# Regrouping the matmul order of a 32-expert block by tile width: one block of full-width work per expert, the sums of a pair as one block, 32-column work ahead of 64-column work in the down projection

## The chip, the cores and the metric

The kernel runs on one core of one Trainium2 chip. The metric is the device time of one execution in microseconds (us). A core has a matmul engine (TensorE, PE in the profile; its weight loads are listed as PEld), three engines for vectors and scalars (VectorE or DVE, ScalarE or ACT, GpSimd or POOL), and SyncE (SP), whose queue issues nearly all loads here. Each engine works through its own queue in order; between engines there are semaphores. The PE writes only to PSUM, eight banks of 512 float32 per partition, and the DVE or the ACT takes the results out.

## The reference, cut to what matters

The program is one layer of a hybrid encoder for 512 tokens of width 1024. A pooling mixer and a differential attention, then a cross-attention, then a mixture of 32 experts (each token goes to four) are added to `x`; a last RMSNorm follows. The change touches only the experts:

```
logits = xt @ w_router + b_router
top_val, top_idx = lax.top_k(logits, 4);  gates = softmax(top_val)
for each expert e, for the tokens that chose it:
    gate, up = split(xb @ w_gu[e] + b_gu[e])
    hb = (min(up, 7) clipped at -7, + 1) * min(gate, 7) * sigmoid(1.702 * gate)
    y[token] += (hb @ w_down[e] + b_down[e]) * gate_weight
```

## The kernel before

**What one expert is.** The kernel gives each expert 96 places (`CAP`); experts with more tokens are finished by a loop at the end (`overflow`), which does nothing in this run. The first 64 places are worked on in matmuls with 64 stationary columns, two of which stand side by side in the array (one fills PSUM partitions 0 to 63, the other 64 to 127). The last 32 places are worked on in matmuls with 32 stationary columns, four side by side. Experts with at most 64 tokens skip most of the 32-column work: the PE branches on a flag (`when`, line 102; `cond()` in the code). All else uses the full 128 columns: gathering a token list (`slots`), turning activations (`xgT`, `actT`), adding biases, and the sums into `x` (`comb`).

**What an iteration of `experts` does.** In iteration `e` of the loop the PE works on gate and up of expert `e` and on the down projection of expert `e - 1`:

- `load_gate_up(e + 1)` and `load_down(e)` put twelve loads of 1 MB on the SP queue, into a pool of 17 buffers.
- `biases` starts the accumulators with the biases: `gu1` (64 places, tile `pa`, a *pair* of two banks) and `gu2` (32 places, tile `pc`, one bank). Both are printed as `gu`.
- `gate_up1(j)`, for `j` from 0 to 7, adds one eighth of the contraction to `gu1` with four 64-column matmuls. Each is recorded as two instructions in the profile, so `x8` there is one `j`.
- `gate_up2(k)` does the same for the 32 places. It stands after `j = 3` (for `k` 0 to 3) and after `j = 7` (for `k` 4 to 7).
- Amid the `j` steps stand, at full width: after `j = 2` `dispatch(e + 2)` (`slots`), after `j = 6` `turn_act` of expert `e - 1` (`actT`), and in odd iterations after each of `j` = 3, 4, 5, 6 one `combine`, which multiplies the weighted results of a *pair* of experts with one-hot matrices for 128 tokens at a time (six matmuls into `comb`) and has the DVE add the sum into `x` (`add_sums`, line 1171 before). There are four such sums for each pair, one for each 128 tokens.
- `swiglu` (lines 1059 to 1065) turns `gu1` and `gu2` into activations on DVE and ACT.
- `to_features` of expert `e + 1` (`xgT`, then two DVE multiplications into `xT`) stands at the end of the gate and up part.
- `down` of expert `e - 1` runs half of its 64-column matmuls (`first(0)`), then its 32-column ones (`second`), then the other half (`first(1)`). ACT and DVE split each result into a high and a low part (lines 120 and 121).

**What sets the order.** On the PE the order is that of the Python code (`queued`, `in_order`): each matmul is issued after the one before it in the program. The other engines' orders are the framework's, which follows readiness.

**PSUM.** Pool `ps1` has four single banks, for `slots`, `actT` (two of them), `gu2`, and the down projection's `down1` and `down2`. Pool `ps2` has two pairs of banks, for `gu1`, `xgT` and `comb`. From the biases to `swiglu`, `gu1` holds one of the two pairs.

Of the kernel before, what the change touches and what calls it, by code (L numbers as in the profile page):

```python
# [23 lines left out]
NT = S // P  # L24
KT = D // P
MEM = 256
NE = 32
# [33 lines left out]
class Block:  # L61
# [1054 lines left out]
    def down(self, aT, aT2, dn, gat, tok, cond, a, c, last=False):  # L1116


        (ya, oha), (yb, ohc) = a, c
        nc, mw = self.nc, self.mw  # L1120
        pd = [self.bank("down1") for _ in range(2)] if last else [self.bank("down1")] * 2
        pe = self.bank("down2", (P, 256))

        def first(h):
            for c in range(4):
                w = dn[2 * h + c // 2]
                for o in range(2):
                    k = D * (c % 2) + 512 * o
                    self.mm(pd[o][64 * o:64 * o + 64], aT[:, c, 64 * h:64 * h + 64], w[:, k:k + 512],
                            start=h == 0 and c == 0, stop=h == 1 and c == 3, skip_group_check=True)  # L1130

        def second(q, b):
            for o in range(4):
                k = D * b + 256 * o
                self.mm(pe[32 * o:32 * o + 32], aT2[:, b, 32 * q:32 * q + 32], dn[q][:, k:k + 256],
                        start=q + b == 0, stop=q == 3 and b == 1, skip_group_check=True)

        nc.vector.tensor_scalar(oha, self.iota_t, tok[:, 0:1], None, op0=OP.is_equal)
        nc.vector.tensor_scalar(ohc, self.iota_t[0:64], tok[0:64, 1:2], None, op0=OP.is_equal)
        if not last:  # L1140
            first(0)
        second(0, 0)
        with cond():
            for k in range(1, 8):
                second(k // 2, k % 2)
        for q in range(4):
            r, c = slice(32 * q, 32 * q + 32), slice(256 * (q % 2), 256 * (q % 2) + 256)
            self.split(yb[0:32, q // 2, c], yb[32:64, q // 2, c], pe[r], scale=gat[r, 1:2])
        if last:
            first(0)  # L1150
        first(1)
        for h in range(2):
            r = slice(64 * h, 64 * h + 64)
            self.split(ya[0:64, h], ya[64:P, h], pd[h][r], scale=gat[r, 0:1])
# [18 lines left out]
    def experts(self):  # L1173
# [7 lines left out]
            return [t[:, 0] for t in disp[e][1:]]  # L1181

        xTs[0] = self.first_features()
        acts, parts = {}, {}
        pick = self.pick.rearrange("p v h q e -> p (v h q) e")
        for e in range(NE + 1):

            if e < NE:
                gu = self.gu.pop(e)
                cond = lambda e=e: self.when(self.flag(e))  # L1190
                if e == 0:
                    biases = self.load_down_biases()
                if e + 1 < NE:
                    self.load_gate_up(e + 1)
                    if e:
# [4 lines left out]
                for j in range(KT):  # L1200
                    self.gate_up1(pa, xT, gu[j], j)
                    if e == 0 and j == 0:
                        self.count()
                    if e == 0 and j == 1:
                        disp[1] = self.dispatch(1, 1)
                        gather(1)
                    if j == 3 or e == 0 and j in (1, 5):
                        with cond():
                            for k in range(j - 1 if e == 0 else 0, j + 1):
                                self.gate_up2(pc, xT, gu[k], k)  # L1210
                    if j in (3, 4, 5, 6) and e % 2 and e > 2:
                        self.combine(j - 3, parts[e // 2 - 1])
                    if j == 2 and e + 2 < NE:
                        disp[e + 2] = self.dispatch(e + 2, 1)
                    if j == 5 and e == 0:
                        disp[0] = self.dispatch(0, 1)
                        biases = self.round_down_biases(biases)
                    if e == 1 and j == 2:
                        biases = self.down_biases(biases)
                    if e == 1 and 2 < j < 7:  # L1220
                        self.combine(j - 3, [biases])
                    if j == 6 and e >= 1:
                        aT = [self.turn_act(t, n) for t, n in zip(acts.pop(e - 1), (4, 2))]
                    if j == 6 and e + 1 < NE:
                        xg = self.normed(xgs.pop(e + 1))
                if e:
                    act = self.swiglu(pa[:, 0], pa[:, 1], 512)
                with cond():
                    for k in range(4 if e else 6, KT):
                        self.gate_up2(pc, xT, gu[k], k)  # L1230
                if e == 0:
                    xTs[1] = self.to_features(xg)
                    act = self.swiglu(pa[:, 0], pa[:, 1], 512)
                acts[e] = act, self.swiglu(pc[:, 0], pc[:, 1], 256)
                if 0 < e < NE - 1:
                    xTs[e + 1] = self.to_features(xg)
            else:
                aT = [self.turn_act(t, n) for t, n in zip(acts.pop(e - 1), (4, 2))]

            if e:  # L1240
                f = e - 1
# [159 lines left out]
```

## Time and profile before

| | |
|---|---|
| time, median of 3 runs | 1530.17 us (1529.25 to 1530.84) |
| time of the profiled execution | 1531.06 us |
| span of its instructions | 1529.3 us |
| granted TensorE clock, mean over the span | 0.989 |
| PE busy | 1482.5 us, 97% |
| DVE, ACT, POOL busy | 695.2, 385.1, 39.0 us |
| read from HBM | 449.45 MB, 297 GB/s over the span |

The expert loop takes the span from about 390 us (biases of expert 0) to about 1500 us. [...]

### The profile page before, as it was taken

Reading aid. Unit: us, or ns where it says so; the run is one execution under the profiler, and the core shown is the slowest. Engines: PE = TensorE matmul, PEld = TensorE weight load, DVE = VectorE, ACT = ScalarE, POOL = GpSimd, SP = SyncE. Lnnn points to the kernel's source line nnn. Section 1 sums busy time; section 2 is a strip of 40 time slices with the busy share of each in tenths; the row PEclk is TensorE's granted clock in tenths of the full one; section 3 lists DMA queues with packets and bytes.
Section 4 is the critical chain, followed back from the end, with each engine's and each line's share of the span. In section 5 each row is a group of like instructions: output and inputs, shape, how many; then the busy total and the mean of one; then the engine's idle time right before and its main releaser. Section 6 shows DMA issues by size and latency. Waiting matters only on the chain. (4 is left out here: it accounts for less than half of the span.)

```text
span 1529.3 us, 22025 instructions
## 1 busy us (share of the span) xinstructions
PE 1482.5 (97%) x8852; PEld 748.6 (49%) x8852; DVE 695.2 (45%) x1679; ACT 385.1 (25%) x691; POOL 39.0 (3%) x52
## 2 busy tenths in 40 slices
PE   8999999999999999999999999999999999999994
PEld 7878788888433333434333333333343433433332
DVE  6858865543353433335343334344343433444234
ACT  5346644441111111121211112121111112121113
POOL 0000000000000000000000000000000000000001
PEclk9999999999899999999999999999999999999997
DMA  6222225148778998989999998899989999999901
GB/s 221 90 86 88 106 63 175 80 196 318 273 304 341 387 398 318 369 356 373 396 405 408 407 381 344 343 400 367 395 342 386 387 393 370 364 396 387 416 25 57
DMA packets 84153, 455.38 MB, mean 298 GB/s; under 512 B 14169, under 2 KB 14690, under 8 KB 34882
## 3 DMA queue, kind: packets, MB, share of 16 engines
q1 hardware_dynamic: 79170, 438.90, 72.9%
q0 software_dynamic: 3472, 12.29, 2.5%
q10 hardware_dynamic: 1392, 2.51, 0.4%
q8 instruction: 87, 1.43, 0.4%
q14 instruction: 32, 0.26, 0.0%
HBM read 449.45 MB, written 4.21 MB: 297 GB/s over the span
## 5 line engine op out<-in xcount | busy, mean ns | idle before, releaser
L107 PE MATMUL gu<-gu,xT 128*64 128x512 f32 (+1 forms) x3200 | 602.7, 598 | 1.3 <-PEq L102 1.3
L107 PEld LDWEIGHTS gu<-gu,xT 128*64 128x64 f32 (+1 forms) x3200 | 167.7, 127 | 344.2 <-issue 337.3
L107 PE MATMUL down<-dnw,aT 128*32 128x256 f32 (+1 forms) x2288 | 305.3, 478 | 3.3 <-PEq L102 2.5
L107 PEld LDWEIGHTS down<-dnw,aT 128*32 128x32 f32 (+1 forms) x2288 | 109.1, 122 | 175.3 <-issue 149.6
L1105 ACT ACTIVATE aT<-actT 128x512 f32<-128x512 f32 x64 | 27.9, 487 | 542.2 <-PE actT L111 542.2
L1171 DVE TENSOR_TENSOR x<-comb,x 128x1024 f32<-128x1024 f32 x68 | 82.9, 1221 | 131.6 <-PE comb L107 131.6
L1059 DVE TENSOR_SCALAR g<-gu 128x256 f32<-128x256 f32 (+1 forms) x64 | 33.3, 554 | 229.1 <-PE gu L107 193.5
L121 DVE SCALAR_TENSOR_TENSOR yb<-down,gat,yb 32x256 fp32r<-32x256 f32 x128 | 61.6, 481 | 129.4 <-ACT yb L120 129.4
L120 ACT ACTIVATE yb<-down,gat 32x256 fp32r<-32x256 f32 x128 | 59.7, 466 | 224.3 <-PE down L107 118.2
L107 PE MATMUL comb<-ya,yb 128*128 128x512 f32 x256 | 97.0, 420 | 3.7 <-PEq L102 2.8
L107 PEld LDWEIGHTS comb<-ya,yb 128*128 128x128 f32 x256 | 47.9, 187 | 63.3 <-DVE x L1171 37.8
L118 DVE TENSOR_TENSOR w_lo<-w,w_hi 128x1024 fp32r<-128x1024 f32 x56 | 67.0, 1219 | 7.5 <-ACT w_hi L117 7.2
L121 DVE SCALAR_TENSOR_TENSOR ya<-down,gat,ya 64x512 fp32r<-64x512 f32 x64 | 48.0, 750 | 26.6 <-ACT ya L120 26.5
L970 DVE COPY slots<-slots 128x12 f32<-128x12 f32 x32 | 5.5, 171 | 118.3 <-PE slots L107 118.3
L117 ACT ACTIVATE w_hi<-w 128x1024 fp32r<-128x1024 f32 x56 | 56.6, 1052 | 5.6 <-DMA w<-in_w_ckv_dram 1.4
L1061 ACT ACTIVATE s<-g 128x256 f32<-128x256 f32 (+1 forms) x64 | 32.4, 521 | 87.6 <-DVE g L1059 85.8
L992 POOL DMA_INDIRECT xg<-x_rows,gi x31 | 28.6, 921 | 1004.2 <-DVE gu L1062 566.1
L120 ACT ACTIVATE ya<-down,gat 64x512 fp32r<-64x512 f32 x64 | 43.8, 685 | 32.6 <-DVE ya L121 23.9
L107 PE MATMUL comb<-yb,ohc 128*128 128x512 f32 x128 | 50.2, 393 | 0.0
L1065 DVE TENSOR_TENSOR g<-gu,s 128x512 f32<-128x512 f32 (+1 forms) x64 | 48.8, 842 | 0.0
L111 PEld LDWEIGHTS xgT<-ident,xg 96*128 96x128 f32 x248 | 29.9, 203 | 30.6 <-ACT xg L999 16.3
L999 ACT ACTIVATE xg<-xg 96x1024 f32<-96x1024 f32 x31 | 35.6, 1149 | 20.2 <-DMA xg<-x_rows,gi 19.5
(339 smaller groups left out, 1754.8 us busy)
## 6 DMA issues: line engine op xcount, KB each, us to landing
gu<-in_w_gu_dram SPq DMA_DIRECT2D x256, 1024.0 KB, 12.5
dnw<-in_w_down_dram SPq DMA_DIRECT2D x128, 1024.0 KB, 9.3
w<-in_w_ckv_dram SPq DMA_DIRECT2D x8, 1024.0 KB, 5.2
w<-in_w_in_dram SPq DMA_DIRECT2D x7, 1024.0 KB, 7.5
w<-in_w_out_dram SPq DMA_DIRECT2D x4, 1024.0 KB, 5.0
w<-in_w_cq_dram SPq DMA_DIRECT2D x4, 1024.0 KB, 7.8
w<-in_w_co_dram SPq DMA_DIRECT2D x4, 1024.0 KB, 5.1
x<-in_x_dram SPq DMA_DIRECT2D x8, 256.0 KB, 6.4
```

The source lines that it names most:

```text
L107: self.pin(self.nc.tensor.matmul(*a, **k))
L111: self.pin(self.nc.tensor.transpose(*a))
L117: self.pin(nc.scalar.activation(hi, src, AF.Copy))
L118: self.pin(nc.vector.tensor_tensor(lo, src, hi.bitcast(F32), op=OP.subtract))
L120: nc.scalar.activation(hi, src, AF.Copy, scale=scale)
L121: nc.vector.scalar_tensor_tensor(lo, src, scale, hi.bitcast(F32), op0=OP.mult, op1=OP.subtract)
L992: nc.gpsimd.indirect_dma_start(out=xg, out_offset=None, in_=self.rows, in_offset=bass.IndirectOffsetOnAxis(ap=gi, axis=0))
L999: self.nc.scalar.activation(xg[:, :D], xg[:, :D], AF.Copy, scale=xg[:, D:D + 1]))
L1059: nc.vector.tensor_scalar(g, gate, LIMIT, None, op0=OP.min)
L1061: nc.scalar.activation(s, g, AF.Sigmoid, scale=ALPHA)
L1065: nc.vector.tensor_tensor(g.rearrange("s (j b p) -> s j p b", p=P, b=2), r(up), r(s), op=OP.mult)
L1171: self.nc.vector.tensor_tensor(xi, ps, xi, op=OP.add)
```

## The change

Nothing is computed that was not computed before, and no load, buffer or tile changes its size. The order of work in an iteration changes:

- `dispatch(e + 2)`, `to_features(e)` and `turn_act` of expert `e - 1` stand together ahead of `biases(e)`. `to_features` moves by this from the end of iteration `e - 1` to the start of iteration `e`.
- The four `combine` of a pair stand together after `gate_up1(3)` and ahead of `gate_up2(0..3)`.
- In iteration 0 the first `swiglu` (of `gu1`) is written ahead of the last `gate_up2`, as in the other iterations. The framework now puts the `gu2` part first on the DVE, and both after the last `gate_up2`.
- `down` runs `second` first, then `first(0)` and `first(1)`.
- In iteration 1 the transposes of the gates and the four sums of the down projection's biases, which stood amid `gate_up1` of expert 1, stand at the start of the iteration, ahead of everything else.

```
-        if not last:
-            first(0)
         second(0, 0)
...
-        if last:
-            first(0)
+        first(0)
         first(1)
...
+            if e == 1:
+                biases = self.down_biases(biases)
+                for i in range(NT):
+                    self.combine(i, [biases])
+            if 0 < e < NE - 2:
+                disp[e + 2] = self.dispatch(e + 2, 1)
+            if 0 < e < NE:
+                xTs[e] = self.to_features(xg)
+            if e:
+                aT = [self.turn_act(t, n) for t, n in zip(acts.pop(e - 1), (4, 2))]
...
+                    if j == 3 and e % 2 and e > 2:
+                        for i in range(NT):
+                            self.combine(i, parts[e // 2 - 1])
                     if j == 3 or e == 0 and j in (1, 5):
                         with cond():
                             for k in range(j - 1 if e == 0 else 0, j + 1):
                                 self.gate_up2(pc, xT, gu[k], k)
-                    if j in (3, 4, 5, 6) and e % 2 and e > 2:
-                        self.combine(j - 3, parts[e // 2 - 1])
-                    if j == 2 and e + 2 < NE:
-                        disp[e + 2] = self.dispatch(e + 2, 1)
...
-                    if e == 1 and j == 2:
-                        biases = self.down_biases(biases)
-                    if e == 1 and 2 < j < 7:
-                        self.combine(j - 3, [biases])
-                    if j == 6 and e >= 1:
-                        aT = [self.turn_act(t, n) for t, n in zip(acts.pop(e - 1), (4, 2))]
...
-                if e:
-                    act = self.swiglu(pa[:, 0], pa[:, 1], 512)
+                act = self.swiglu(pa[:, 0], pa[:, 1], 512)
...
-                if 0 < e < NE - 1:
-                    xTs[e + 1] = self.to_features(xg)
```

What this makes of the PE's queue in an odd iteration, from the first sum on, before (`ya`, `yb` and `ohc` hold the weighted results and the one-hot matrices of a pair; `comb` is the sum in PSUM; `32x512` and `64x512` are shapes of results, so 32-column and 64-column work):

```order
L107 MATMUL comb<-ya,yb 128x512
L107 MATMUL comb<-yb,ohc 128x512
L107 MATMUL comb<-ya,yb 128x512 x2
L107 MATMUL comb<-yb,ohc 128x512
L107 MATMUL comb<-ya,yb 128x512
L107 MATMUL gu_4373<-gu,xT 64x512 x4
L107 MATMUL comb<-ya,yb 128x512
L107 MATMUL comb<-yb,ohc 128x512
L107 MATMUL comb<-ya,yb 128x512 x2
L107 MATMUL comb<-yb,ohc 128x512
L107 MATMUL comb<-ya,yb 128x512
L107 MATMUL gu_4373<-gu,xT 64x512 x4
```

The same place after the change, the first sum and the second:

```order
L107 MATMUL gu_4410<-gu,xT 64x512 x16
L107 MATMUL comb<-ya,yb 128x512
L107 MATMUL comb<-yb,ohc 128x512
L107 MATMUL comb<-ya,yb 128x512 x2
L107 MATMUL comb<-yb,ohc 128x512
L107 MATMUL comb<-ya,yb 128x512 x2
L107 MATMUL comb<-yb,ohc 128x512
L107 MATMUL comb<-ya,yb 128x512 x2
L107 MATMUL comb<-yb,ohc 128x512
```

Between two sums there is no other matmul any more; the last matmul of one sum and the first of the next are printed as one row of two.

The DVE's queue at that place after the change (`x<-comb,x` is the addition into `x`):

```order
L1010 TENSOR_TENSOR xT<-xgT,g_ffn 128x384
L121 SCALAR_TENSOR_TENSOR ya<-down_4771,gat,ya 64x512
L961 TENSOR_SCALAR oh<-iota_2383,slot_no 128x256 x2
L1074 CAST lh<-pick 128x384
L1168 TENSOR_TENSOR x<-comb,x 128x1024 x3
L1139 TENSOR_SCALAR ohc<-iota_t,tok 64x512
L102 UNCONDITIONAL_BRANCH
L1168 TENSOR_TENSOR x<-comb,x 128x1024
```

Nothing stands between the additions of the first three sums.

The end of an iteration and the start of the next on the PE, before:

```order
L111 MATMUL xgT<-ident,xg 128x96 x8
L107 MATMUL down_4548<-dnw,aT_4488 64x512 x8
L107 MATMUL down_4549<-dnw,aT_4493 32x256 x4
L102 REGISTER_ALU
L102 COMPARE_AND_BRANCH
L107 MATMUL down_4549<-dnw,aT_4493 32x256 x28
L102 UNCONDITIONAL_BRANCH x2
L107 MATMUL down_4548<-dnw,aT_4488 64x512 x8
L107 MATMUL gu_4643<-bias,lh 128x512 x2
L107 MATMUL gu_4646<-bias,lh 128x512 x2
L107 MATMUL gu_4643<-gu,xT 64x512 x12
```

And after the change, from the last of the eight `slots` matmuls on:

```order
L107 MATMUL slots<-tv,oh 128x6
L111 MATMUL xgT<-ident,xg 128x96 x8
L111 MATMUL actT<-ident,g 128x128 x6
L107 MATMUL gu_4410<-bias,lh 128x512 x2
L107 MATMUL gu_4413<-bias,lh 128x512 x2
L107 MATMUL gu_4410<-gu,xT 64x512 x16
```

The transposes `xgT` and `actT` now stand directly ahead of the biases and of `gate_up1`, which reads what the DVE makes of `xgT`.

## Rows read from the trace of the kernel before

**Rows 1.** The page, part 1: busy time and share of the span by engine.

```profile
PE 1482.5 (97%) x8852; PEld 748.6 (49%) x8852; DVE 695.2 (45%) x1679; ACT 385.1 (25%) x691; POOL 39.0 (3%) x52
```

**Rows 2.** Waits of the PE, longest in total first: total us, times, longest us.

```profile
PE comb L107 <- PEq L102: 3.1, 10, 0.3
```

**Rows 3.** Timeline of the PE, iteration 12: start us, length us, instructions.

```profile
791.84 1.20 PE L107 MATMUL gu<-bias,lh 128*128 128x512 f32 x4
792.96 5.37 PE L107 MATMUL gu<-gu,xT 128*64 128x512 f32 x24
798.27 0.35 PE L107 MATMUL slots<-tv,oh 128*128 128x6 bf16 x8
798.55 10.81 PE L107 MATMUL gu<-gu,xT 128*64 128x512 f32 x64
809.29 0.88 PE L111 MATMUL actT<-ident,g 128*128 128x128 f32 x6
810.10 5.51 PE L107 MATMUL gu<-gu,xT 128*64 128x512 f32 x40
815.54 1.13 PE L111 MATMUL xgT<-ident,xg 96*128 96x96 f32 x8
816.59 4.22 PE L107 MATMUL down<-dnw,aT 128*64 128x512 f32 x24
821.00 3.65 PE L107 MATMUL down<-dnw,aT 128*64 128x512 f32 x16 [0.18 <-PEq L102]
824.58 1.21 PE L107 MATMUL gu<-bias,lh 128*128 128x512 f32 x4
```

**Rows 4.** Timeline of the PE, iteration 13, the second of its four sums.

```profile
835.10 1.94 PE L107 MATMUL gu<-gu,xT 128*64 128x512 f32 x8
836.97 0.50 PE L107 MATMUL comb<-ya,yb 128*128 128x512 f32 x1
837.31 0.40 PE L107 MATMUL comb<-yb,ohc 128*128 128x512 f32 x1
...
838.25 0.40 PE L107 MATMUL comb<-ya,yb 128*128 128x512 f32 x1
838.57 1.94 PE L107 MATMUL gu<-gu,xT 128*64 128x512 f32 x8
```

**Rows 5.** Timeline of the DVE, iteration 13; the last row groups a line's instructions.

```profile
825.41 0.74 DVE L121 SCALAR_TENSOR_TENSOR ya<-down,gat,ya 64x512 fp32r<-64x512 f32 x1 [0.40 <-ACT ya L120]
...
831.41 0.17 DVE L970 COPY slots<-slots 128x12 f32<-128x12 f32 x1 [3.75 <-PE slots L107]
...
832.43 0.29 DVE L961 TENSOR_SCALAR oh<-iota,slot_no 128x256 bf16<-128x256 bf16 x1
...
838.68 1.23 DVE L1171 TENSOR_TENSOR x<-comb,x 128x1024 f32<-128x1024 f32 x1 [2.25 <-PE comb L107]
...
L1010 DVE TENSOR_TENSOR xT<-xgT,g_ffn 128x384 f32<-128x384 f32 x62 | 31.2, 544 | 0.0
```

**Rows 6.** Timeline at the end (`finish`): a DVE addition, and the sum awaiting it.

```profile
1504.52 1.22 DVE L1171 TENSOR_TENSOR x<-comb,x 128x1024 f32<-128x1024 f32 x1 [0.59 <-PE comb L107]
...
1505.80 0.50 PE L107 MATMUL comb<-ya,yb 128*128 128x512 f32 x1 [0.85 <-DVE x L1171]
```

**Rows 7.** Timeline around the start of iteration 1, PE and DVE.

```profile
418.72 5.37 PE L107 MATMUL gu<-gu,xT 128*64 128x512 f32 x24
...
419.26 1.53 DVE L1065 TENSOR_TENSOR g<-gu,s 128x512 f32<-128x512 f32 x2
...
425.94 0.68 DVE L953 TENSOR_TENSOR gT<-gT 32x512 fp32r<-32x512 f32 x1
427.76 1.23 DVE L1171 TENSOR_TENSOR x<-comb,x 128x1024 f32<-128x1024 f32 x1 [1.14 <-PE comb L107]
```

**Rows 8.** Stretches: bounds, length, busy by engine (instructions), granted clock, DMA share, GB/s.

```profile
1505.00:1510.00 5.00, 3.06 (x12) 2.17 (x12) 4.38 (x5) 3.43 (x6) 2.99 (x2) 1.00 0.00 0
1510.00:1515.00 5.00, 0.00 (x0) 0.00 (x0) 4.79 (x8) 1.15 (x2) 4.01 (x2) 0.66 0.03 7
```

More of the change, by code (lines that the diff above doesn't have):

```diff
@@ L1183, in experts @@
         xTs[0] = self.first_features()
-        acts, parts = {}, {}
+        acts, parts, xg = {}, {}, None
         pick = self.pick.rearrange("p v h q e -> p (v h q) e")
         for e in range(NE + 1):
+            if e == 0:
+                biases = self.load_down_biases()
+            if e == 1:
[8 more added lines that the diff above has]
+                aT = [self.turn_act(t, n) for t, n in zip(acts.pop(e - 1), (4, 2))]
             if e < NE:
@@ L1190, in experts @@
                 cond = lambda e=e: self.when(self.flag(e))
-                if e == 0:
-                    biases = self.load_down_biases()
                 if e + 1 < NE:
@@ L1210, in experts @@
                                 self.gate_up2(pc, xT, gu[k], k)
-                    if j in (3, 4, 5, 6) and e % 2 and e > 2:
-                        self.combine(j - 3, parts[e // 2 - 1])
-                    if j == 2 and e + 2 < NE:
-                        disp[e + 2] = self.dispatch(e + 2, 1)
+                    if e == 0 and j == 2:
+                        disp[2] = self.dispatch(2, 1)
                     if j == 5 and e == 0:
@@ L1230, in experts @@
                         self.gate_up2(pc, xT, gu[k], k)
-                if e == 0:
-                    xTs[1] = self.to_features(xg)
-                    act = self.swiglu(pa[:, 0], pa[:, 1], 512)
                 acts[e] = act, self.swiglu(pc[:, 0], pc[:, 1], 256)
-                if 0 < e < NE - 1:
-                    xTs[e + 1] = self.to_features(xg)
-            else:
-                aT = [self.turn_act(t, n) for t, n in zip(acts.pop(e - 1), (4, 2))]
             if e:
```

## The prediction

> **What bounds the kernel now.** I read the page's busy shares first: the PE is busy 97% of the span, the next engine 45% [rows 1]. Then the waits of the PE: the longest entry is 3.1 us in ten pieces, and it is the branch on an expert's flag, no other engine and no load [rows 2]. So the expert loop is one queue of matmuls, and only two things can change the time: what the matmuls cost in their order, and waits that the new order puts into the queue. For the first I read the starts in one iteration, not the lengths, because matmuls overlap.
>
> A group of two 64-column (or four 32-column) matmuls follows the one before after 0.429 us: 24 instructions take 5.37 us and 8 take 1.94, so eight pairs make the difference of 3.43 [rows 3]. Iteration 12 has 64 such groups (32 of `gu1`, 16 of `gu2`, 16 of `down1`), 27.46 us. To these come two groups of half the length (0.43), four biases at 0.235, the spacing of full-width matmuls in [rows 4] (0.94), eight `slots` (about 0.2), and six and eight transposes about 0.11 apart (1.54). Together that is 30.57 us. The iteration takes 32.74, from biases to biases [rows 3]. The rest is 2.17 us. About 0.2 of it is the skipped branch in `down` (0.18 idle in its row). The other 1.97 fall on 13 places at which the tile width changes: **0.15 us a change of width**. The sums of iteration 13 give the same from the other side: from one `gu` group to the next are 3.47 us, less 1.72 for four pairs and 1.40 for six matmuls leaves 0.35 for two changes, 0.175 each [rows 4]. `slots` gives the lower end: from 792.96 twelve pairs reach 798.11, `gu` goes on at 798.55, and less 0.2 of `slots` that leaves 0.24, or 0.12 each [rows 3].
>
> **The change, part by part.**
>
> *Fewer changes of width: a gain.* With 32-column work, an even iteration has 13 changes now and 6 afterwards (into the block of full-width work, out of it, 64 to 32, back, 64 to 32 for `gu2` and straight on into `second`, back to 64 for `first`). An odd one has 18 now, since the sums go in and out four times, and 7 afterwards. Without 32-column work it is 10 and 4, and 16 and 6. A pair of iterations loses 16 to 18, and there are 15 pairs from iteration 2 to 31: 255 x 0.15 = 38 us (31 at 0.12, 45 at 0.175). The trace of before doesn't show three new neighbours in each iteration: `slots` to `xgT`, `actT` to biases, and `gu2` to `second` over a branch. None changes the width. They cost between nothing and a change's 0.15: 0 to 13 us for 90 of them; I take 3, near the end of no change, because the array's width stays.
>
> [...] The rows have 0.12 to 0.175, so I go by the rows.
>
> *The sums as one block: a new wait.* `comb` lives in `ps2`, which has two pairs of banks, and `gu1` holds one of them from the biases to `swiglu`. All four sums of a pair therefore use the other. A sum can't start before the DVE has added the one before it into `x`. Now this addition (1.23 us) runs beside four pairs of `gu` (1.72 us) and costs nothing. Afterwards nothing stands between the sums, the PE's queue is in order, and behind the waiting matmul are the rest of the sums, `gate_up2` and everything after. From the rows: the last matmul of a sum starts at 838.25, the addition at 838.68 [rows 4, 5], so 0.43 later. It lasts 1.23. At the end of the kernel a sum waits for just such an addition: that one ends at 1505.74 and the matmul starts at 1505.80 [rows 6], 0.06 later. So the next sum starts 1.72 us after the last matmul, in place of 0.235: 1.48 us of wait. The second matmul after a fresh start follows after 0.34 and not 0.235 [rows 4], another 0.1. That is **1.59 us for each of three sums in each of 15 pairs: 71 us** (67 without the 0.1). The first sum of a block waits for nothing; the addition of the fourth runs beside later matmuls. Nothing else stands between the DVE's first three additions, so it can't be later than this either.
>
> *The block at the start of an iteration.* `gate_up1` now reads `xT` soon after `xgT`. On the PE, `slots`, `xgT`, `actT` and the biases take 0.28 + 1.05 + 0.81 + 1.12 us with one change of width in each [rows 3]; without three of these it is about 2.9 from the first `slots`. The DVE copies `slots` 0.39 after their start, works about 1.0 on them until the lists are made (831.41 to 832.43), does one split of `ya` (0.74) that stands in between, and the first half of `xT` (0.54): 2.7 us [rows 3, 5]. That just fits: I take 0, with 0.3 a block (9 us) as the upper end. `swiglu`, which must be through before `actT`, has all of `down1` as cover (16 groups of 0.43, 6.9 us); its last two multiplications take 1.53 us [rows 7] and the six operations ahead of them less than that for each two.
>
> *Iteration 1: a wait, once.* Its biases' sums now stand ahead of everything. The DVE finishes `swiglu` of expert 0 at about 419.7 (it ended at 420.8 with two halves of `xT` between, 1.1 us, which are later now [rows 5, 7]), then needs some 1.1 for `gT` (0.68 for its longer part), and four additions of 1.23, the first of which starts 0.77 after its sum of two matmuls (0.34 + 0.43): about 426.5. Four one-hots (0.29 each, overlapping, 0.8) follow, then the block of 2.9 us. `gate_up1` starts near 430 and not at 418.72 [rows 7]: 11.3 us. In return `slots` (0.44), `gT` (as much), four sums (0.47 + 0.35 each) and `actT` (0.81, less a change that it shares) no longer interrupt it: 4.8 us. Loss: 6.5 us (4 to 8). The PE stands idle there for nearly 5 us. [...]
>
> *Loads.* The last sums release the first `gu` buffers about 10 us later in an odd iteration. No PE wait is a load now, and iterations get longer on average, so I take 0.
>
> **Sum:** -38 + 3 + 71 + 0 + 6.5 + 3 = +46 us (45.5). The profiled execution took 1531.06 us, its span 1529.3, and lies 0.9 above the median of the runs. 1531.1 + 45.5 - 0.9 gives 1576 us.
>
> **The rivals.**
>
> 1. *The sums don't wait, or less.* If additions and sums overlapped, there would be only -38 + 3 + 6.5 + 3: 1505 us, faster. It turns at 0.57 us a wait (25.5 us over 45). For it: the four sums wait nowhere now. Against it: one free pair of banks, and at the end a sum starts only after the whole addition [rows 6]. 5%.
> 2. *Waits and gain cancel.* A wait of about 0.6 us at the same place, for instance if a sum's first bank were free as soon as half of the addition is done, with the gain at its upper end of 45: within 3 us of 1530. Against it speaks the same row. 3%.
> 3. *The clock falls in each block of sums.* Its 24 matmuls (5.6 us) would take twice as long, 15 x 5.6 = 84 us more: 1660 us. It decides if the granted clock of these stretches is under 1. Against it: from 1505 to 1510 the PE was busy for 3.06 of 5 us, with one such wait, at a clock of 1.00 [rows 8]. [...] 7%.
>
> That the change doesn't do what it says is no rival: the PE's queue has the sums in one block.
>
> **How the numbers follow.** The forecast has 85%, the rivals 5, 3 and 7. With all terms at their favourable ends: -45 + 0 + 67 + 0 + 4 + 0 = +26, 1556 us. At the other ends: -31 + 13 + 72 + 9 + 8 + 7 = +78, 1608; not all fall together, so the range ends at 1600. That leaves out 15% for the rivals and some 4% of the forecast's own. A measurement of this kernel can tell about 0.2% (3 us) from no change: faster 5%, same 3%, slower 92%.
>
> **What the profile afterwards would show.** In an odd iteration the sums should stand 3.0 us apart, each but the first behind an idle time of about 1.3 us that a DVE addition into `x` ends; the waits of the PE should list this with 45 entries in all. An even iteration should be about 1 us shorter. The clock should stay at 1.00 between 440 and 1500 us. I would be wrong if the sums followed each other at 1.4 us, if even iterations got longer (the new neighbours or `xT` cost more than I took), or if the clock fell.

## The result, and the profile after

The changed kernel takes 1576.14 us in the median of four runs (1572.89 to 1576.35); the kernel before, run beside it on the same chip, took 1530.51 us. The ratio is 1.0289, with a 95% interval of 1.0266 to 1.0312: 2.9% slower. The forecast was 1576. The profiled execution took 1576.12 us, its span 1574.3 us.

The page of the changed kernel, parts 1 and 5 (line, engine, operation, out<-in, count | busy us, mean ns | idle us of the engine just before, and what ended most of it):

```profile
PE 1462.3 (93%) x8852; PEld 770.6 (49%) x8852; DVE 701.2 (45%) x1679; ACT 389.1 (25%) x691; POOL 38.9 (2%) x52
...
L107 PE MATMUL comb<-ya,yb 128*128 128x512 f32 x256 | 97.1, 420 | 60.1 <-DVE x L1168 60.1
L1168 DVE TENSOR_TENSOR x<-comb,x 128x1024 f32<-128x1024 f32 x68 | 82.7, 1221 | 156.7 <-PE comb L107 156.7
```

The PE does the same 8852 matmuls as in [rows 1] with 20 us less of busy time, yet its share falls from 97 to 93%. The rows below say where the gap is: 60.1 us of idle time stand in front of the matmuls of the sums, and all of it ends with the DVE's addition into `x` (line 1168 now). The waits of the PE in the changed kernel (total us, times, longest) list it first, 47 times: 45 times in the blocks of sums, 1.32 us each, once in iteration 1 and once at the end of the kernel. In [rows 2] the longest entry was a branch:

```profile
PE comb L107 <- DVE x L1168: 60.6, 47, 1.3
PE down L107 <- PEq L102: 6.5, 27, 0.3
PE comb L107 <- DVE gT L953: 5.2, 1, 5.2
```

An odd iteration, timeline of the PE in the changed kernel (start us, length us; in brackets the idle time before, and what ended it), from the first `slots` of iteration 13 to the gate-up matmuls behind the sums, and the biases of iteration 14:

```profile
845.04 0.35 PE L107 MATMUL slots<-tv,oh 128*128 128x6 bf16 x8
845.25 1.11 PE L111 MATMUL xgT<-ident,xg 96*128 96x96 f32 x8
846.20 0.82 PE L111 MATMUL actT<-ident,g 128*128 128x128 f32 x6
846.78 1.18 PE L107 MATMUL gu<-bias,lh 128*128 128x512 f32 x4
848.09 7.09 PE L107 MATMUL gu<-gu,xT 128*64 128x512 f32 x32
855.11 0.50 PE L107 MATMUL comb<-ya,yb 128*128 128x512 f32 x1
...
856.37 0.40 PE L107 MATMUL comb<-ya,yb 128*128 128x512 f32 x1
858.09 0.50 PE L107 MATMUL comb<-ya,yb 128*128 128x512 f32 x1 [1.32 <-DVE x L1168]
...
861.06 0.50 PE L107 MATMUL comb<-ya,yb 128*128 128x512 f32 x1 [1.32 <-DVE x L1168]
...
864.04 0.50 PE L107 MATMUL comb<-ya,yb 128*128 128x512 f32 x1 [1.32 <-DVE x L1168]
...
865.85 7.09 PE L107 MATMUL gu<-gu,xT 128*64 128x512 f32 x32
...
885.58 1.18 PE L107 MATMUL gu<-bias,lh 128*128 128x512 f32 x4
```

The DVE at the same place:

```profile
856.81 1.23 DVE L1168 TENSOR_TENSOR x<-comb,x 128x1024 f32<-128x1024 f32 x1 [6.66 <-PE comb L107]
859.78 1.23 DVE L1168 TENSOR_TENSOR x<-comb,x 128x1024 f32<-128x1024 f32 x1 [1.75 <-PE comb L107]
```

The two engines take turns. The last matmul of the first sum starts at 856.37, the addition starts at 856.81 and ends at 858.04, and the next sum starts at 858.09. The sums stand 2.97 us apart, where six matmuls at the spacing of [rows 4] take 1.40. Iteration 13 takes 38.80 us (846.78 to 885.58); it took 35.60 before. Iteration 12, without sums, takes 31.80 (814.98 to 846.78), against 32.74 [rows 3].

For all kernels below it helps to cut the span at two marks, the starts of the biases of expert 0 and of expert 2, read from each profiled execution. The first stretch holds iterations 0 and 1, the second iterations 2 to 31 and what follows. In the kernels with the block at an iteration's start, eight `slots` and six `actT` of iteration 2 (0.21 and 0.58 us in the rows above) have moved ahead of the second mark, so 0.8 us of the first stretch is moved work there (in e11 too).

| kernel | biases 0 | biases 2 | end | first stretch | second stretch |
|---|---|---|---|---|---|
| before | 390.31 | 449.93 | 1529.28 | 59.6 | 1079.4 |
| changed | 390.06 | 461.78 | 1574.29 | 71.7 | 1112.5 |
| e1, sums apart again | 389.06 | 458.77 | 1518.97 | 69.7 | 1060.2 |
| e2, before with the block of sums | 390.43 | 451.35 | 1589.47 | 60.9 | 1138.1 |
| e3, half sums in single banks | 388.54 | 458.08 | 1499.46 | 69.5 | 1041.4 |
| e4, iteration 1's sums amid gate-up | 388.77 | 452.36 | 1565.05 | 63.6 | 1112.7 |
| e5, e3 and e4 | 391.00 | 455.79 | 1497.42 | 64.8 | 1041.6 |
| e6, matmuls in iteration 1's idle time | 390.49 | 459.48 | 1572.28 | 69.0 | 1112.8 |
| e7, e4 and sums apart | 390.17 | 453.70 | 1513.90 | 63.5 | 1060.2 |
| e8, before with the order in down | 388.43 | 447.93 | 1522.35 | 59.5 | 1074.4 |
| e9, e5 with four matmuls apart | 388.37 | 451.67 | 1547.60 | 63.3 | 1095.9 |
| e10, e5 with the same four together | 389.32 | 453.84 | 1500.33 | 64.5 | 1046.5 |
| e11, e5 with iteration 1 as before | 390.20 | 451.65 | 1493.24 | 61.5 | 1041.6 |

Kernels with the same order in iterations 2 to 31 agree in the second stretch within 0.3 us (the changed kernel, e4 and e6; e1 and e7; e3, e5 and e11). The second stretch is therefore a sharper measure than the whole time, which carries the part ahead of the first mark (388.37 to 391.00 us).

The first stretch is less sharp, and part of its differences is no effect of any edit. From the biases of expert 0 to the third group of eight `slots` all kernels have the same order on the PE. That part took 19.1 to 19.4 us in eight of the traces, 19.9 in e10's, and 20.5 to 20.6 in those of the changed kernel, e2, e5 and e11, among them e2, whose iteration 0 is that of the kernel before. What differs, in the three traces read for it, is when the granted clock comes back from 0.50, at which it stands ahead of the first mark: at 392 us in the kernel before, between 394 and 395 (0.71 there) in the changed kernel, and in e11 its mean from 392 to 396 is 0.68. The kernel before, a stretch (bounds, length, busy of PE, PEld, DVE, ACT, POOL, granted clock, DMA share, GB/s), the last `gate_up1` of iteration 0, and the start of the `swiglu` that follows it:

```profile
392.00:396.00 4.00, 4.00 (x21) 1.13 (x20) 1.67 (x11) 0.00 (x0) 0.00 (x0) 1.00 0.00 0
...
409.86 5.51 PE L107 MATMUL gu<-gu,xT 128*64 128x512 f32 x32
...
415.43 1.02 DVE L1059 TENSOR_SCALAR g<-gu 128x256 f32<-128x256 f32 x2 [2.48 <-PE gu L107]
```

And in the changed kernel, whose `swiglu` starts at 416.54 (its row stands further down):

```profile
382.00:394.00 12.00, 12.00 (x45) 9.93 (x46) 2.26 (x7) 1.26 (x2) 0.00 (x0) 0.50 0.45 172
...
410.96 5.51 PE L107 MATMUL gu<-gu,xT 128*64 128x512 f32 x32
```

In both, `swiglu` starts 5.6 us after the start of that last row. Counted from the third `slots`, the rest of the first stretch is 40.35 us before, 51.10 in the changed kernel, 50.40 and 50.33 in e1 and e3, which have the same iterations 0 and 1, 44.2 and 44.3 in e4 and e5, 49.89 in e6 and 40.90 in e11.

### The profile page after: what moved, and what is told of

It is laid out like the page before. It is cut to its first block, busy times and chain, and to the rows that moved or that the text cites. A ratio compares the mean times of both kernels' runs of the same rounds, so it can differ in the third digit from the quotient of the medians.

```text
span 1574.3 us, 21995 instructions
## 1 busy us (share of the span) xinstructions
PE 1462.3 (93%) x8852; PEld 770.6 (49%) x8852; DVE 701.2 (45%) x1679; ACT 389.1 (25%) x691; POOL 38.9 (2%) x52
## 5 line engine op out<-in xcount | busy, mean ns | idle before, releaser
L107 PE MATMUL gu<-gu,xT 128*64 128x512 f32 (+1 forms) x3200 | 584.5, 597 | 4.7 <-PEq L102 1.5
L107 PEld LDWEIGHTS gu<-gu,xT 128*64 128x64 f32 (+1 forms) x3200 | 181.3, 127 | 382.5 <-issue 367.4
L107 PE MATMUL down<-dnw,aT 128*32 128x256 f32 (+1 forms) x2288 | 300.1, 476 | 7.4 <-PEq L102 6.5
L107 PEld LDWEIGHTS down<-dnw,aT 128*32 128x32 f32 (+1 forms) x2288 | 120.8, 122 | 183.5 <-issue 157.8
L1059 DVE TENSOR_SCALAR g<-gu 128x256 f32<-128x256 f32 x64 | 32.7, 552 | 391.4 <-PE gu L107 284.7
L107 PE MATMUL comb<-ya,yb 128*128 128x512 f32 x256 | 97.1, 420 | 60.1 <-DVE x L1168 60.1
L1061 ACT ACTIVATE s<-g 128x256 f32<-128x256 f32 x64 | 33.5, 523 | 468.4 <-DVE g L1059 467.9
L120 ACT ACTIVATE yb<-down,gat 32x256 fp32r<-32x256 f32 x128 | 59.6, 466 | 126.2 <-DVE yb L121 87.1
L1065 DVE TENSOR_TENSOR g<-gu,s 128x256 f32<-128x256 f32 x64 | 49.2, 843 | 3.0 <-ACT s L1061 3.0
L1105 ACT ACTIVATE aT<-actT 128x512 f32<-128x512 f32 x64 | 31.2, 491 | 43.6 <-PE actT L111 42.9
L107 PE MATMUL gu<-bias,lh 128*128 128x512 f32 x128 | 39.5, 432 | 0.0
L111 PE MATMUL xgT<-ident,xg 96*128 96x96 f32 x248 | 34.8, 284 | 0.0
```

The source lines that it names most:

```text
L107: self.pin(self.nc.tensor.matmul(*a, **k))
L111: self.pin(self.nc.tensor.transpose(*a))
L120: nc.scalar.activation(hi, src, AF.Copy, scale=scale)
L1059: nc.vector.tensor_scalar(g, gate, LIMIT, None, op0=OP.min)
L1061: nc.scalar.activation(s, g, AF.Sigmoid, scale=ALPHA)
L1065: nc.vector.tensor_tensor(g.rearrange("s (j b p) -> s j p b", p=P, b=2), r(up), r(s), op=OP.mult)
```

## The experiments

The theory was: `ps2` has one free pair of banks for the sums, so each sum behind another waits for a DVE addition (71 us in all), while fewer changes of tile width give 38 us back. The rivals were that the block at the start of an iteration costs the time, or the clock, or that the sums overlap.

**e1: the sums apart again.** The changed kernel with the four sums after `j` = 3 to 6 as before, all else as changed.

```
-                    if j == 3 and e % 2 and e > 2:
-                        for i in range(NT):
-                            self.combine(i, parts[e // 2 - 1])
...
+                    if j in (3, 4, 5, 6) and e % 2 and e > 2:
+                        self.combine(j - 3, parts[e // 2 - 1])
```

> The changed kernel with one part undone: the four sums of a pair stand again after gate_up1 of j = 3, 4, 5, 6; the block at the start of an iteration, the order in down and iteration 1 stay changed. Theory (a sum waits for the addition of the one before it, 1.59 us, 45 times, and a change of width costs 0.15 us): the waits go, 6 changes of width come back in each of 15 pairs: 1576 - 71 + 13.5 = 1518 us (1512 to 1524); the PE's waits list no DVE addition in the pairs. Rival (the block at the start of an iteration and its new neighbours cost the time, the sums little): 1565 us or more.

Measured: 1521.96 us, ratio 0.9948 (0.9931 to 0.9964). That is 54 us below the changed kernel, and faster than the kernel before. Timeline of its PE in iteration 13, the second of the four sums:

```profile
836.27 1.94 PE L107 MATMUL gu<-gu,xT 128*64 128x512 f32 x8
838.14 0.50 PE L107 MATMUL comb<-ya,yb 128*128 128x512 f32 x1
...
839.42 0.40 PE L107 MATMUL comb<-ya,yb 128*128 128x512 f32 x1
839.74 1.94 PE L107 MATMUL gu<-gu,xT 128*64 128x512 f32 x8
```

No sum of a pair waits for an addition in the loop any more: four pairs of `gu` stand between two sums and cover it. The block at the start of an iteration is still in this kernel and costs nothing net; that rival falls.

**e2: the block of sums alone, in the kernel before.**

```
+                    if j == 3 and e % 2 and e > 2:
+                        for i in range(NT):
+                            self.combine(i, parts[e // 2 - 1])
                     if j == 3 or e == 0 and j in (1, 5):
...
-                    if j in (3, 4, 5, 6) and e % 2 and e > 2:
-                        self.combine(j - 3, parts[e // 2 - 1])
```

> The kernel before with one part of the change alone: the four sums of a pair as one block after gate_up1(3), ahead of gate_up2. Theory: 45 waits of 1.59 us, 71 us, less 4 changes of width in each of 15 pairs, 9 us: 1530 + 62 = 1592 us (1586 to 1598), slower than the whole change. Rival (the block at the start of an iteration costs the time): 1520 to 1530 us.

Measured: 1590.15 us, ratio 1.0391 (1.0374 to 1.0409). This one part costs more than the whole change. The first wait of its PE:

```profile
PE comb L107 <- DVE x L1171: 60.1, 46, 1.3
```

It is the same entry (45 waits in the blocks and the one at the end), without the block at the iteration's start and without anything new in iteration 1. The second stretch is 58.8 us longer than before.

**e3: half a sum in a single bank.** The changed kernel, with each sum of a pair split into two halves of 512 columns. A half goes into one bank of `ps1` (four banks, one of which `gu2` holds, so three are free) and has its own addition; the PE does the same matmuls in the same places, grouped by half.

```
+    def combine_halves(self, i, parts):
+        t = slice(i * P, (i + 1) * P)
+        for h in range(2):
+            ps = self.bank("comb")
+            for k, (y, oh) in enumerate(parts):
+                self.mm(ps, oh[:, t], y[h] if isinstance(y, list) else y[:, h], start=k == 0,
+                        stop=k == len(parts) - 1, skip_group_check=True)
+            xi = self.x_sb[:, i, 512 * h:512 * h + 512]
+            self.nc.vector.tensor_tensor(xi, ps, xi, op=OP.add)
...
-                            self.combine(i, parts[e // 2 - 1])
+                            self.combine_halves(i, parts[e // 2 - 1])
```

> The changed kernel, with what makes a sum wait taken away: each half of a sum (512 columns, three matmuls) has a single bank of the other pool, of which three are free there, and its own DVE addition of 512 columns; the PE's order stays. Theory (the one free pair of banks makes the wait): units of three matmuls take 0.7 us on the PE and about as much on the DVE, so nearly all 45 waits go: 1576 - 71 + 0 to 8 = 1505 to 1513 us. Rival (a sum costs more in the block for another reason than its banks, or the clock is low there): 1565 us or more.

Measured: 1504.14 us, ratio 0.9836 (0.982 to 0.9853), a little below the range that I expected. The groups of the sums on its page:

```profile
L1167 DVE TENSOR_TENSOR x<-comb,x 128x512 f32<-128x512 f32 x120 | 82.7, 689 | 91.6 <-PE comb L107 91.0
...
L107 PE MATMUL comb<-ya,yb 128*128 128x512 f32 x256 | 85.4, 404 | 0.9 <-DVE x L1179 0.9
```

The sums stay together, the DVE adds as much data as before, now in 120 halves, and 60.1 us of idle time have become 0.9, which stand at the end of the kernel. What makes the sums wait is the one free pair of banks, not that they stand together. The edit gives them more buffers and smaller ones at once; whole sums in two free pairs were not tried, so what the size does by itself isn't shown. The second stretch is 71.1 us shorter than that of the changed kernel, 1.58 us for each of 45 waits.

**e4: iteration 1's sums amid gate-up.** The changed kernel, with the gate transposes and the four sums of the biases back at their old places.

```
-            if e == 1:
-                biases = self.down_biases(biases)
-                for i in range(NT):
-                    self.combine(i, [biases])
...
+                    if e == 1 and j == 2:
+                        biases = self.down_biases(biases)
+                    if e == 1 and 2 < j < 7:
+                        self.combine(j - 3, [biases])
```

> The changed kernel with iteration 1 undone in part: the gate transposes and the four sums of the down projection's biases stand again amid gate_up1 of expert 1. Theory (they wait for swiglu of expert 0 and for their own additions, and the clock falls): 1576 - 12 = 1564 us (1561 to 1568), and the granted clock stays at 1.00 from 395 us to 1500. Rival (the idle time there is covered by work that would wait anyhow): 1573 us or more.

Measured: 1567.63 us, ratio 1.0253 (1.0236 to 1.027): 8.5 us below the changed kernel. The first stretch is 8.1 us shorter, and 6.9 of that stand behind the third `slots` of iteration 0. I expected 1564, with the clock at 1.00 throughout. Its PE and a stretch (columns as above) show what I missed:

```profile
414.10 1.11 PE L111 MATMUL xgT<-ident,xg 96*128 96x96 f32 x8
418.45 1.51 PE L111 MATMUL actT<-ident,g 128*128 128x128 f32 x6 [3.24 <-DVE slots L970]
...
418.00:422.00 4.00, 3.55 (x12) 2.53 (x14) 2.08 (x11) 0.38 (x1) 0.00 (x0) 0.57 0.80 284
```

With the sums away, `actT` is the next to wait for the same DVE work, `swiglu` of expert 0, since no down projection stands in iteration 0 to cover it. (Its row names a copy of 0.17 us, L970; that copy and `swiglu` both end at 418.31.) The granted clock is 1.00 from 416 to 418 us, amid that idle time, 0.57 in the mean of 418 to 422, and 1.00 from 422 to 424.

**e5: e3 and e4 together** (the two edits above).

> The changed kernel with the halves of a sum in single banks (as in e3_halves) and with iteration 1's gate transposes and biases' sums amid gate_up1 again (as in e4_iter1_amid). Theory (the two costs have nothing to do with each other, so they add): 1504.1 - (1576.1 - 1567.6) = 1496 us (1492 to 1500). Rival (they overlap, what one leaves the other takes up): 1502 us or more.

Measured: 1495.57 us, ratio 0.9773 (0.9757 to 0.979). The two gains add up: the second stretch is that of e3, the first, from the third `slots` on, that of e4.

**e6: matmuls in the idle time of iteration 1.** The changed kernel with 80 small matmuls more, whose results are not used.

```
                 biases = self.down_biases(biases)
+                self.warm(80)
                 for i in range(NT):
                     self.combine(i, [biases])
```

> The changed kernel with 80 small matmuls (into a PSUM bank of their own, their results are not used) put into the start of iteration 1, ahead of the sums of the biases, where the PE stands idle for 5.2 us. In the changed kernel the granted clock is 0.50 from 421.9 to 435.5 us there. Theory: the idle time lets the clock fall, and with matmuls in it the clock stays at 1.00 there; what stands in this stretch at full clock loses about half of its length, of which the sums wait on the DVE anyway: 3 us less than the changed kernel, 1573. Rival: the clock falls for another reason, or what is at half clock there hides behind the DVE: 1576 within 1. If the added matmuls themselves delay the first sum: up to 1579.

Measured: 1574.17 us, ratio 1.0279 (1.0265 to 1.0292). The interval overlaps that of the changed kernel, so the time decides nothing. Timeline of its PE, and its stretches:

```profile
415.76 4.63 PE L107 MATMUL warm<-ones 128*128 128x128 bf16 x80
421.19 1.16 PE L107 MATMUL comb<-b_down,gT 96*128 96x512 f32 x4 [0.80 <-DVE gT L953]
...
424.00:426.00 2.00, 0.73 (x2) 0.30 (x2) 2.00 (x3) 0.00 (x0) 0.00 (x0) 0.99 0.00 0
426.00:428.00 2.00, 1.18 (x11) 0.93 (x12) 2.00 (x9) 0.00 (x0) 0.00 (x0) 0.50 0.00 0
```

The 5.2 us of idle time are filled, and the clock falls all the same, four microseconds later, to 0.50 from 426 to 432, in the stretch in which the sums of the biases wait for their additions. So the one idle time that I named does not decide the clock here. What the lower level costs in iteration 1 stays open: from the third `slots` on, the first stretch is 1.2 us shorter than in the changed kernel, but only 0.4 to 0.5 us shorter than in e1 and e3, which have no such matmuls.

**e7: before with the block at the iteration's start and the order in down,** sums and iteration 1's biases as before (e4 with the edit of e1).

> The kernel before with two parts of the change: the block at the start of an iteration and the new order in down; the sums of a pair and iteration 1 stay as before. Theory: 1522.0 - 8.5 (what e4_iter1_amid won back) = 1513.5 us, 1.1% faster than before; e5_halves_iter1 lies 17 us below it, since its block of sums saves six changes of width in each of 15 pairs (13.5 us). Rival (changes of width about the sums are not what makes the block good): both within 5 us.

Measured: 1515.22 us, ratio 0.9901 (0.9885 to 0.9918). The second stretch is 1060.2 us as in e1, the first 63.5 as in e4. e5 lies 19.7 us below it, where I expected 17, so the rival (within 5) falls.

**e8: the kernel before with the order in down alone** (`second` ahead of both `first`).

> The kernel before with one part of the change alone: in the down projection the 32-column matmuls stand ahead of all 64-column ones. Theory: 15 or 16 experts run their 32-column work, and each loses one change of tile width at the place in the middle (64 to 32 and back becomes one change after the 32-column gate and up work is through, or after xgT): 31 skipped or run branches aside, about 30 changes at 0.15 us, 4.6 us, 1525.5. Rival (a change at this place costs nothing, since the branch already parts the work): 1530 within 1.

Measured: 1524.53 us, ratio 0.9957 (0.9945 to 0.9969). The second stretch is 4.9 us shorter, with 31 changes of width fewer in it (403 instead of 434, counted in the trace): 0.16 each. The rest of the 6.9 us between the medians stands mostly ahead of the first mark, which comes 1.9 us earlier, so it is no effect of this edit.

**e9 and e10: more changes of width with the same work.** Both are e5 with four small full-width matmuls more in each iteration from 2 on, results unused. In e9 they stand one by one amid `gate_up1`, in e10 together ahead of the biases, where no change of width is added; so the time expected of e10 is the same whatever a change costs.

```
                 pa, pc = self.biases(pick[:, :, e:e + 1])
+                extra = self.bank("extra")
                 for j in range(KT):
                     self.gate_up1(pa, xT, gu[j], j)
...
+                    if e > 1 and j in (0, 1, 5, 6):
+                        self.mm(extra[:, :P], self.ones, self.ones, start=True, stop=True)
```

> e5_halves_iter1 with four extra full-width matmuls (128 columns, bfloat16, into a bank that nobody reads) in each of iterations 2 to 31, each amid 64-column work: after j = 0, 1, 5 and 6 of gate_up1. It adds 120 times two changes of width and a short matmul. Theory (0.15 us a change): e10_same_width + 240 x 0.15 = 36 us (29 to 42). [...]

> The counterpart of e9_more_widths: the same four extra matmuls in each of iterations 2 to 31, but together ahead of the biases, among full-width work. No change of width is added. Both theories: e5_halves_iter1 + 120 x 0.06 = 7 us.

Measured: e9 1549.95 us, ratio 1.0135 (1.0118 to 1.0152); e10 1501.53 us, ratio 0.9813 (0.9797 to 0.983). The difference of 48.4 us is above what I expected, and the iterations say why. Those without sums take 33.05 us in e9 and 32.00 in e10 (31.80 in e5): 1.05 us for eight changes, 0.13 each. Those with sums differ by 2.0 to 2.3 us. Timelines of e9's PE, one of the added matmuls in an iteration without sums, and half sums in one with:

```profile
800.44 1.94 PE L107 MATMUL gu<-gu,xT 128*64 128x512 f32 x8
802.31 0.23 PE L107 MATMUL extra<-ones 128*128 128x128 bf16 x1
802.47 1.94 PE L107 MATMUL gu<-gu,xT 128*64 128x512 f32 x8
...
841.26 0.50 PE L107 MATMUL comb<-ya,yb 128*128 128x512 f32 x1
...
842.53 0.98 PE L107 MATMUL comb<-ya,yb 128*128 128x512 f32 x2
843.35 0.40 PE L107 MATMUL comb<-yb,ohc 128*128 128x512 f32 x1
...
848.34 3.87 PE L107 MATMUL gu<-gu,xT 128*64 128x512 f32 x16
```

From 800.44 to 802.47 are 2.03 us, less 1.72 for four groups [rows 3]: 0.31 for a matmul and two changes. In the block of sums every other half now takes 0.35 us longer than in e3, 7.08 us for the block (841.26 to 848.34). In e3 it took 6.01: its PE there,

```profile
827.58 0.50 PE L107 MATMUL comb<-ya,yb 128*128 128x512 f32 x1
...
833.59 7.09 PE L107 MATMUL gu<-gu,xT 128*64 128x512 f32 x32
```

The added tile `extra` holds one of the four banks of `ps1` until `j = 6` in e9 and `gu2` another, so two are left to the half sums. The traces bear it out: in e9 the third half starts at 843.01, when the first half's addition has ended (842.96); in e3 it starts at 829.08, while that addition still runs (until 829.28). 15 blocks at 1.07 make 16 us; of the 49.4 us between the second stretches 33.4 remain for 240 changes: 0.14 each, in agreement with the iterations without sums. The pair was meant to measure the change alone, and in the odd iterations it did not.

**e11: e5 with iteration 1 wholly as before:** `slots` after `j = 2`, `actT` after `j = 6`, `xgT` of expert 1 at the end of iteration 0.

```
-            if 0 < e < NE - 2:
+            if 1 < e < NE - 2:
                 disp[e + 2] = self.dispatch(e + 2, 1)
-            if 0 < e < NE:
+            if 1 < e < NE:
                 xTs[e] = self.to_features(xg)
-            if e:
+            if e > 1:
                 aT = [self.turn_act(t, n) for t, n in zip(acts.pop(e - 1), (4, 2))]
...
-                    if e == 0 and j == 2:
-                        disp[2] = self.dispatch(2, 1)
+                    if e < 2 and j == 2:
+                        disp[e + 2] = self.dispatch(e + 2, 1)
...
+                    if e == 1 and j == 6:
+                        aT = [self.turn_act(t, n) for t, n in zip(acts.pop(0), (4, 2))]
...
-                act = self.swiglu(pa[:, 0], pa[:, 1], 512)
+                if e:
+                    act = self.swiglu(pa[:, 0], pa[:, 1], 512)
...
+                if e == 0:
+                    xTs[1] = self.to_features(xg)
+                    act = self.swiglu(pa[:, 0], pa[:, 1], 512)
```

> The version with half sums in single banks and iteration 1's sums of the biases amid gate_up1, and now also the rest of iteration 1 as in the kernel before: slots after j = 2, actT after j = 6, xgT of expert 1 at the end of iteration 0. Iterations 2 to 31 keep the changed order. From the biases of expert 0 to those of expert 2 the kernel before took 59.6 us, the version without this step 64.8, with 3.2 us of idle time in which actT waits for the DVE's work on expert 0. Theory: the block at the start of iteration 1 is what costs these 5.2 us, since nothing (no down projection) stands there to hide swiglu of expert 0: about 1490.5 us, 59.6 us from biases 0 to biases 2, and the granted clock at 1.00 from 396 to 1420 us. Rival: the wait only moves (xgT or the biases then wait for the same DVE work): 1495 within 1.5.

Measured: 1494.21 us, ratio 0.976 (0.9747 to 0.9773), the lowest time of all. From e5 its interval can't be told apart, and the time lies in the rival's range, not at the 1490.5 of the theory. The trace decides: the first stretch is 3.3 us shorter. I expected 5.2, and had overlooked the 0.8 us of moved work and 1.2 us that iteration 0 took more in e5 than in the trace of the kernel before, where the first eight `gu` took 1.94 us and in e5 3.04; e11's iteration 0 was as long as e5's. Its PE and stretches:

```profile
418.80 1.16 PE L107 MATMUL gu<-bias,lh 128*128 128x512 f32 x4 [1.21 <-DVE xT L1010]
...
416.00:440.00 24.00, 22.18 (x126) 8.63 (x122) 14.62 (x31) 3.53 (x6) 0.92 (x1) 1.00 0.75 297
```

The idle time of 3.2 us has become the 1.21 us that the kernel before had too, and the clock stays at 1.00 in iteration 1.

## Why the prediction was right

The total was 0.2 us off. That close it is luck, though its parts are right: between the two traces the waits measure 71.1 us (forecast 71), the changes of width with their new neighbours -37.2 (forecast -35), iteration 1 10.0 (forecast 9.5), and 1.1 us come from the clock ahead of that and from the part ahead of the first mark, which nobody forecast. The errors nearly cancel.

**The wait of the sums: right in mechanism and size.** Forecast 1.59 us for each of 45 waits, 71 us. In the changed kernel the last matmul of a sum and the first of the next start 1.72 us apart (856.37 and 858.09), as worked out from [rows 4, 5, 6], and e3 takes 71.1 us off the second stretch. The 60.6 us of the list are the idle time alone; the rest lies in the last matmul's own length and in the slower second matmul. e2 shows the cost alone, e1 its absence.

**Fewer changes of width: right.** The traces count 434 changes in iterations 2 to 31 before and 181 after, 253 fewer where I had 255. With the waits gone (e3), the second stretch is 38.0 us shorter than before, and 37.2 with the moved work put back. The forecast was 38 less 3 for new neighbours. An even iteration is 0.94 us shorter, forecast about 1. The new neighbours and the gain are not separated; together they came out 2 us better than forecast. The price of a change is 0.13 us amid 64-column work (e9), 0.16 in `down` (e8), and at the sums (18.8 us for the 90 changes between e1 and e3) 0.21, or 0.18 without the 2.8 us that e1 waits at a branch ahead of the first sum. The prediction's 0.12 to 0.175 holds all but the last.

What happens in the array at a change is not shown by any run. e9 and e10 show the price apart from the new order: 33 us for 240 changes, 0.14 each, after the blocks of sums are taken out.

**The block at the start of an iteration: nearly nothing, as taken.** In iteration 13 the first `gu` starts 1.31 us after the biases (1.19 in the even iterations), where iteration 12 before had 1.12 [rows 3]. At most 0.2 us of each block is a wait for `xT`; the upper end was 0.3.

**Iteration 1: right in sign and size, the clock's share put in the wrong place.** Forecast 6.5 + 3 us. The first stretch grew by 11.3 (71.7 against 59.6, less 0.8 of moved work), but 1.3 of that stand ahead of the third `slots` of iteration 0, in the same code. From there on it is 10.0 in the changed kernel, and 9.2 to 9.3 in e1 and e3 with the same two iterations. The changed kernel, PE and DVE:

```profile
416.54 1.02 DVE L1059 TENSOR_SCALAR g<-gu 128x256 f32<-128x256 f32 x2 [3.18 <-PE gu L107]
...
422.25 2.04 PE L107 MATMUL comb<-b_down,gT 96*128 96x512 f32 x4 [5.24 <-DVE gT L953]
...
426.02 2.35 DVE L1168 TENSOR_TENSOR x<-comb,x 128x1024 f32<-128x1024 f32 x2 [0.18 <-PE comb L107]
...
428.62 0.88 PE L107 MATMUL slots<-tv,oh 128*128 128x6 bf16 x8 [1.52 <-DVE oh L961]
...
433.81 7.93 PE L107 MATMUL gu<-gu,xT 128*64 128x512 f32 x32
```

The DVE begins `swiglu` 1.1 us later than in the trace before (416.54 against 415.43), by the late clock in iteration 0 and not by the new order, and ends it at 420.94. The last addition ends at 428.37 where I had 426.5, 0.8 us more than that delay explains. One step of the sum was misplaced: from `slots` to `gate_up1` are 5.19 us where I had 2.9, with the granted clock at 0.50. No run shows the last 3 us of the sum (0 to 7 at its ends), which stood for the clock: the first row of `gate_up1`, on which I had put them, is 0.84 us longer (7.93 against the 7.09 of the same row in iteration 13). So `gate_up1` starts at 433.81 instead of 430. How much of all this is the clock isn't separated. e4 shows that 6.9 us hang on where the sums of the biases stand.

**The rivals.** The sums don't overlap (rival 1), and a sum's first bank isn't free before the addition has ended: 858.04 and 858.09 (rival 2). The clock (rival 3), by stretches of the changed kernel:

```profile
422.00:424.00 2.00, 1.75 (x4) 1.16 (x4) 0.62 (x2) 0.00 (x0) 0.00 (x0) 0.50 0.09 37
...
435.00:436.00 1.00, 1.00 (x6) 0.15 (x4) 0.00 (x0) 0.17 (x1) 0.00 (x0) 0.73 0.08 21
436.00:438.00 2.00, 2.00 (x12) 0.69 (x10) 0.00 (x0) 0.97 (x1) 0.00 (x0) 1.00 0.00 0
...
440.00:1500.00 1060.00, 993.33 (x6153) 412.06 (x6148) 409.97 (x927) 190.51 (x329) 26.50 (x29) 1.00 0.92 366
```

From 440 to 1500 us it is 1.00, across all blocks of sums but the last, which starts at 1499.3; from 1500 to 1512 it is 1.00 as well. The idle times in a block stand three in a row, 1.32 us each, and the clock stays (1.00 from 786 to 799 and from 855 to 866, two such blocks). The rival's factor of two is nearer 1.8: the last two biases of iteration 1 start 0.43 us apart at a clock of 0.50 (432.82 and 433.25), full-width matmuls of the same size 0.235 apart at 1.00 [rows 4].

The gain of 37 us was there and was outweighed by the waits for one buffer. With the sums halved into free banks (e3) the same regrouping is 1.6% faster than the kernel before, and with iteration 1 left as it was (e11) 2.4%.

## What to carry to other kernels

Before work is put together into a block, ask which buffer its pieces share and who empties it: pieces that stood apart may have had the engine that empties them hidden by what stood between. Such a block needs as many buffers as let the emptying run behind. Halving the piece gave them here without more memory, since it let the sums use single banks of the other pool that stood free, and the emptying engine kept up. A regrouping that pays in each iteration of a loop can still lose in the first, where the work that covered its inputs does not exist yet.

## What the runs showed of the hardware

- A change of tile width cost 0.13 us of start spacing (e9, between 64 columns and full width), 0.16 (e8, between 64 and 32 in `down`) and 0.18 to 0.21 (e1 against e3, at the sums). It doesn't show as idle time: in e9 the added matmul starts at 802.31, and the row ahead of it (800.44, 1.94 long) ends at 802.38, so the PE counts as busy. The spacing of starts told it.
- In iteration 1 the granted clock fell about the end of idle times of the PE of 3.24 us (e4: 1.00 from 416 to 418, 0.57 from 418 to 422) and 5.24 us (the changed kernel: 0.94 from 421 to 422, 0.50 from 422 to 435), and also without any idle time over 1.8 us, amid four shorter ones of 0.80, 0.85, 0.40 and 1.73 us (e6: 0.99 from 424 to 426, 0.50 from 426 to 432). It stayed at 1.00 over the blocks of sums with three idle times of 1.32 us each (the changed kernel, 440 to 1500). In the changed kernel the PE had no idle time from 428.6 us until the clock came back at about 435.5 (0.73 from 435 to 436).
- The granted clock stood at its lower level while the PE counted as busy all the time: 0.50 from 380 to 391 us in the kernel before, with the PE busy for 11.00 of 11.00 us (full-width float32 matmuls with 96 result columns, `xgT` of expert 0). It was 1.00 from 392 us in the kernel before and from 395 in the changed kernel, with the same order on the PE there; from the biases of expert 0 to the third `slots` took 19.1 to 20.6 us in the traces. Why it fell there stays open.
- Additions of 512 columns from PSUM took 0.69 us each (e3), those of 1024 columns 1.22 us (the changed kernel): half the size cost a little over half, and the DVE's 120 half additions of e3 kept up with the PE on three free banks (0.9 us idle ahead of the matmuls of the sums, all at the end of the kernel). On two (e9) every other half sum came 0.35 us later.
